# Strassen's seven products for the first matrix product of a feed-forward layer

## The chip, the cores and the metric

The kernel runs on one core of a Trainium2 chip. The metric is the device time of one execution in microseconds (us). The engines of the core are TensorE (PE in the profile; PEld is its weight load), VectorE (DVE), ScalarE (ACT), GpSimd (POOL) and SyncE (SP), which issues DMA transfers. Each works through its own list of instructions in order and waits on semaphores for the others.

## The reference

The program is one step of a hybrid encoder layer for two groups of requests with the same weights: one stream of 512 positions and eight streams of 16, 640 tokens in all. D is 1024, the hidden width 2816. The change touches only the last part of the layer:

```python
hf = rmsnorm(x, lw['norm_ffn'])
u, gf = jnp.split(hf @ lw['w_up'], 2, axis=-1)
gf, f_conv_new = causal_dwconv(gf, f_conv, lw['f_conv_w'], lw['f_conv_b'])
x = x + (u * jax.nn.silu(gf)) @ lw['w_down']
```

The convolution has three taps along the positions; f_conv_new holds each stream's last two inputs of it. A final RMSNorm of x follows.

## The kernel before

**Products in three passes.** Values are float32, and TensorE is given float32r operands. An operand a is held as ah (a rounded, a copy by ScalarE) and al = a − ah (a subtraction). A product is the sum of ah·bh, ah·bl and al·bh, so one product with a contraction of 128 is three matmul instructions. For weights, ScalarE makes wh and GpSimd wl from a raw tile that SyncE's queue loads (512 KB each, tag raw, two buffers; wh and wl have six buffers each, 128x512).

**The FFN.** The 2816 hidden columns are 22 factors f of 128. X is the normed input, transposed, in eight parts k of 128 features by 640 tokens. For each f, fmj makes the gate (fps) and then the up product (ups): eight k, three passes, two halves of 320 tokens, so 48 matmul instructions each, into a pair of PSUM banks (PD, tag D, two buffers of two banks; PP, tag P, has four of one). Behind the gate, conv and silu_conv run: ScalarE copies the PSUM into xp, VectorE does the three taps into xc, ScalarE a tanh, VectorE the gate (fs). Behind the up product, VectorE multiplies fs with ups, and split makes hh (ScalarE) and hl (VectorE). lt collects the last inputs of the convolution for f_conv_new (GpSimd).

After f = 7 and f = 15, add_proj multiplies eight factors by w_down (dn, 240 matmul instructions of 512 columns, through wmj) and adds the result to x; after f = 21, last_proj does the other six and the final norm. For f = 0, fmj (split) does the first 320 tokens ahead of the others, so that it begins before the sample streams (token tile 4) are normed.

**Order.** The program is written in one order; each engine's order comes from a scheduler that follows the program and the buffers, and the semaphores are placed by it. A tile of a pool is given out again when all its readers are done. Dependencies inside a PSUM pair go by the tile.

Of the kernel before, what the change touches and what calls it, by code (L numbers as in the profile page):

```python
# [44 lines left out]
class Enc:  # L45
# [1688 lines left out]
    def ffn(self, x, X):
        I, O = self.I, self.O
        wu, wd = I["w_up"][0], I["w_down"][0]
        lt = None
        for f0, n in ((0, 8), (8, 8), (16, 6)):
            H = []
            for f in range(f0, f0 + n):  # L1740
                nb = 4 if f < 20 else 2
                if f % 4 == 0:
                    lt = self.Q("lt")
                s = []

                def gate(ps, f=f, lt=lt, nb=nb, s=s):
                    s.append(self.silu_conv(ps, "f", f, 2, [self.vc("fcw", i * NFF + f) for i in range(3)],
                                            self.vc("fcb", f), (lt, f % 4, nb), "fs"))
                    yield
                    if f % 4 == nb - 1:  # L1750
                        self.store_conv((lt, 0, nb), [(f - f % 4 + i) * P for i in range(nb)], 2,
                                        O["ffn_conv_prompt"], O["ffn_conv_sample"])

                def up(ps, s=s):
                    t = s[0]
                    sv = t.rearrange("p (a b) -> p a b", a=2)
                    self.tt(sv, sv, ps[:, :, :HALF], ALU.mult)
                    h, l = self.U("hh", F32R), self.U("hl", F32R)
                    self.split(h, l, t)
                    H.append((h, l))  # L1760
                first = f == 0
# [2 lines left out]
            if f0 + n < NFF:
                yield from self.add_proj(wd, H, x, k0=f0, nk=n, nm="dn")
            else:
                yield from self.last_proj(wd, H, x, f0, n)
# [31 lines left out]
    def run(self):  # L1799
        I = self.I  # L1800
        all_ = lambda gen: [None for _ in gen]
        x0 = [self.load_x(0)]
# [140 lines left out]
        _, X = to
        self.drive(self.norm_T(x, g, to, ((0, 1), (2, 3))))
        self.need("WS")
        all_(self.norm_T(x, g, to, ((4,),)))
        all_(self.ffn(x, X))

# [46 lines left out]
```

## Time and profile before

| | us |
|---|---|
| median of 3 runs | 1786.48 |
| lowest and highest | 1783.69, 1791.82 |
| the profiled execution | 1787.08 |
| its span, first to last instruction | 1785.4 |

The span lacks the 1.7 us around the first and last instruction. The FFN fills its end: the first product of f = 0 starts at 1303.0, dn stands at 1422.6 and 1589.9, and the last dn starts at 1729.25.

### The profile page before, as it was taken

What the parts mean: (1) busy time and instruction counts of PE and PEld (TensorE: products, weight loads), DVE (VectorE), ACT (ScalarE), POOL (GpSimd) and SP (SyncE); (2) the same over time, 40 slices, a digit from 0 to 9 for tenths busy, and PEclk for the clock granted to TensorE, in tenths of its full rate; (3) what the DMA queues carried; (4) which work ended last, traced back from release to release, by engine and by line L of the source; (5) the groups of instructions that cost most, each with busy time, mean ns of one, the idle gap of its engine ahead of it and who ended that gap; (6) DMA issues with size and microseconds to landing.
All of it is one profiled execution on the core that took longest, in us unless ns stands there. A gap on an engine that the chain in (4) does not pass through costs nothing.

```text
span 1785.4 us, 32450 instructions
## 1 busy us (share of the span) xinstructions
PE 1683.1 (94%) x12925; PEld 1542.6 (86%) x12925; DVE 860.4 (48%) x1762; ACT 650.5 (36%) x1596; POOL 607.4 (34%) x641
## 2 busy tenths in 40 slices
PE   5898999999999998999999899999889999999997
PEld 4687778898988898998899889987789989998995
DVE  5046762446787674755434463243574404431433
ACT  4234543433434432343342245342443313321332
POOL 3252232123322353453432326201144434443432
PEclk9999999999999999999999999999989999999999
DMA  5332156322222334335323345146332222222221
GB/s 177 89 80 66 40 174 197 131 68 64 78 78 67 109 107 113 85 99 145 84 60 119 106 130 166 59 166 236 114 100 74 83 71 83 72 74 82 72 94 61
DMA packets 232749, 181.78 MB, mean 102 GB/s; under 512 B 14321, under 2 KB 198646, under 8 KB 232470
## 3 DMA queue, kind: packets, MB, share of 16 engines
q1 hardware_dynamic: 210672, 165.74, 30.5%
q10 hardware_dynamic: 21926, 13.96, 2.5%
q8 instruction: 102, 1.67, 0.4%
q14 instruction: 49, 0.40, 0.1%
HBM read 163.09 MB, written 16.06 MB: 100 GB/s over the span
## 4 chain that ended last, share of the span: by engine, by line
PE 69%; DVE 10%; DMA 4%; ACT 3%; issue 2%; POOL 1%; ACTq 0%; SPq 0%; POOLq 0%; DVEq 0%
PE ups L235 9%; PE fps L235 9%; PE gps L235 8%; PE dn L235 8%; PE pps L235 6%; PE ap L235 5%; PE tm L235 4%; PE qps L235 3%; PE cps L235 2%; DVE xc L246 2%; PE bps L235 2%; PE pl L235 1%; DVE t L243 1%; PE py L235 1%; PE xkt L240 1%
## 5 line engine op out<-in xcount | busy, mean ns | idle before, releaser
L243 POOL TENSOR_TENSOR wl<-raw,wh 128x512 fp32r<-128x512 f32 x373 | 490.8, 1321 | 961.3 <-ACT wh L249 791.3
L249 ACT ACTIVATE wh<-raw 128x512 fp32r<-128x512 f32 x400 | 248.8, 629 | 591.0 <-PE fps L235 93.8
L246 DVE SCALAR_TENSOR_TENSOR xc<-xp,vec,xc 128x664 f32<-128x664 f32 (+1 forms) x116 | 117.4, 1012 | 3.2
L235 PE MATMUL gps<-xTh,wh 128*128 128x320 f32 x448 | 117.4, 340 | 0.0
L235 PE MATMUL gps<-xTh,wl 128*128 128x320 f32 x448 | 106.3, 315 | 0.0
L235 PE MATMUL gps<-xTl,wh 128*128 128x320 f32 x448 | 105.6, 315 | 0.0
L568 DVE TENSOR_SCALAR xc<-xp,vec 128x656 f32<-128x656 f32 (+1 forms) x34 | 32.2, 948 | 131.9 <-ACT xp L249 131.9
L235 PE MATMUL dn<-wl,hh 128*128 128x512 f32 x220 | 86.4, 394 | 2.9 <-POOL wl L243 2.6
L235 PE MATMUL dn<-wh,hh 128*128 128x512 f32 x220 | 86.3, 393 | 0.1
L235 PE MATMUL dn<-wh,hl 128*128 128x512 f32 x220 | 85.8, 391 | 0.0
L235 PEld LDWEIGHTS gps<-xTh,wh 128*128 128x128 f32 x448 | 74.1, 192 | 12.0 <-issue 10.8
L235 PE MATMUL fps<-fTh,wh 128*128 128x320 f32 x352 | 82.3, 311 | 0.0
L235 PE MATMUL ups<-fTh,wl 128*128 128x320 f32 x352 | 82.0, 310 | 0.0
L235 PE MATMUL fps<-fTl,wh 128*128 128x320 f32 x352 | 81.9, 310 | 0.0
L235 PE MATMUL fps<-fTh,wl 128*128 128x320 f32 x352 | 81.9, 310 | 0.0
L235 PE MATMUL ups<-fTl,wh 128*128 128x320 f32 x352 | 81.8, 310 | 0.0
L235 PE MATMUL ups<-fTh,wh 128*128 128x320 f32 x352 | 81.7, 310 | 0.0
L235 PEld LDWEIGHTS gps<-xTh,wl 128*128 128x128 f32 x448 | 76.0, 190 | 1.0 <-issue 0.8
L235 PEld LDWEIGHTS gps<-xTl,wh 128*128 128x128 f32 x448 | 76.1, 191 | 0.7 <-issue 0.6
L235 PE MATMUL tm<-wh,xTh 128*128 128x256 f32 (+1 forms) x200 | 65.5, 327 | 8.6 <-ACT wh L249 4.4
L243 DVE TENSOR_TENSOR x<-x,dn 128x512 f32<-128x512 f32 x30 | 19.3, 683 | 108.1 <-PE dn L235 107.7
L235 PE MATMUL tm<-wh,xTl 128*128 128x256 f32 (+1 forms) x200 | 63.6, 318 | 0.2 <-DVE xTl L243 0.2
(521 smaller groups left out, 4434.5 us busy)
## 6 DMA issues: line engine op xcount, KB each, us to landing
raw<-in_w_in_dram SPq DMA_DIRECT2D x72, 512.0 KB
raw<-in_w_up_dram SPq DMA_DIRECT2D x44, 512.0 KB
raw<-in_w_down_dram SPq DMA_DIRECT2D x22, 512.0 KB
ck<-in_cache_attn_k_dram SPq DMA_DIRECT2D x32, 256.0 KB
cv<-in_cache_attn_v_dram SPq DMA_DIRECT2D x32, 256.0 KB
xck<-in_cache_mem_k_dram SPq DMA_DIRECT2D x32, 256.0 KB
xcv<-in_cache_mem_v_dram SPq DMA_DIRECT2D x32, 256.0 KB
raw<-in_wx_o_dram SPq DMA_DIRECT2D x14, 512.0 KB
```

What stands on the lines that cost most here:

```text
L235: self.nc.tensor.matmul(out, lhsT=lhsT, rhs=rhs, start=start, stop=stop)
L240: self.nc.tensor.transpose(out, in_, self.ident[b:b + k, b:b + k])
L243: return (eng or self.nc.vector).tensor_tensor(out, a, b, op=op)
L246: self.nc.vector.scalar_tensor_tensor(out, a, s, b, op0=op0, op1=op1)
L249: self.nc.scalar.activation(out, in_, f, **kw)
L568: nc.vector.tensor_scalar(acc[:, :n], xp[:, :n], taps[0], bias, op0=ALU.mult, op1=ALU.add)
```

## The change

The first product is made by the Winograd form of Strassen's algorithm. The contraction is cut in two (k 0 to 3, 4 to 7), the tokens in two (320 each), and the two rows of blocks are the up columns and the gate columns of one f. Seven products of half the contraction by 320 tokens replace eight, so 84 matmul instructions a factor replace 96. For that:

- ffn_weights loads the two raw tiles of a factor and makes four sums of weights on VectorE (ws: s1 to s4, 128x512); half_w makes h and l of seven operands rather than four.
- norm_S replaces norm_T. It holds three blocks of the normed input (b11, b21, b22) and four sums of blocks (t1 to t4; tile tq) as h and l, made in three groups of token tiles.
- ffn_products makes the seven products, two of them at a time in the halves of an fps pair, three in single banks (fpc). VectorE puts their sums together (fo, fu) and writes the gate straight into xp.
- ffn_gate is the convolution and the gate as a generator in steps, advanced once per product. ScalarE does the first tap. The factors of w_down follow after f = 4, 8, 12 and 16, four at a time, and six at the end.
- ffn makes each weight operand LW = 3 products ahead of its use. The products b11 and b21 of f = 0 and 1 come ahead of the rest.
- wmj takes one PSUM pair and three single banks for its five tiles, where it took two pairs and one.

```diff
+LW = 3
@@ wmj
         tiles = list(tiles)
-        acc = []
-        for i in range(0, len(tiles) - 1, 2):
-            ps = self.PD(nm)
-            acc += [(tiles[i], ps[:, 0]), (tiles[i + 1], ps[:, 1])]
-        if len(tiles) % 2:
-            acc.append((tiles[-1], self.PP(nm)))
+        ps = self.PD(nm)
+        acc = [(t, ps[:, i] if i < 2 else self.PP(nm)) for i, t in enumerate(tiles)]
@@ norm_S
+            groups = ((0, 2), (1, 3), (4,))
+            for gi, tiles in enumerate(groups):
+                if gi == 2:
+                    self.need("WS")
+                r = self.token_norm([x[t] for t in tiles])
+                yield FR
...
+                for n, v in (("b11", b11), ("b21", b21), ("b22", b22)):
+                    h, l = QT[n]
+                    for i in range(2):
+                        self.act(h[i][:, :, s], v[:, 2 * i:2 * i + 2, :])
+                        self.tt(l[i][:, :, s], v[:, 2 * i:2 * i + 2, :], h[i][:, :, s].bitcast(F32), ALU.subtract)
+                T = [self.U("tf", shape=(P, 4, w)) for _ in range(4)]
+                self.act(T[2], b12)
+                self.tt(T[0], T[2], b11, ALU.subtract)
+                self.tt(T[1], b22, T[0], ALU.subtract)
+                self.tt(T[2], b22, T[2], ALU.subtract)
+                self.tt(T[3], b21, T[1], ALU.subtract)
+                for i in (1, 0, 2, 3):
+                    h, l = QT[f"t{i + 1}"]
+                    self.act(h[:, :, s], T[i])
+                    self.tt(l[:, :, s], T[i], h[:, :, s].bitcast(F32), ALU.subtract, nc.gpsimd)
@@ half_w, seven, ffn_weights
+        self.act(h, x)
+        self.tt(l, x, h.bitcast(F32), ALU.subtract, eng or self.nc.gpsimd)
...
+        for k in range(4):
+            (wh, wl), (xh, xl) = w[k], q[k]
+            for p, (a, b) in enumerate(((wh, xh), (wh, xl), (wl, xh))):
+                self.mm(ps, a, b, start=(k == 0 and p == 0), stop=(k == 3 and p == 2))
...
+        up, gate = self.raw(wu, f * P, P, 0, NK), self.raw(wu, FF + f * P, P, 0, NK)
+        a11, a12, a21, a22 = up[:, :4], up[:, 4:], gate[:, :4], gate[:, 4:]
+        s1, s2, s3, s4 = (self.U("ws", shape=(P, 4, P)) for _ in range(4))
+        self.tt(s1, a21, a22, ALU.add)
+        self.tt(s2, s1, a11, ALU.subtract)
+        self.tt(s3, a11, a21, ALU.subtract)
+        self.tt(s4, a12, s2, ALU.subtract)
+        for x in (a11, a12, a22, s2, s3, s1, s4):
+            yield self.half_w(x)
@@ ffn_products
+        ps = self.PD("fps")
+        ps = [ps[:, i, :HALF] for i in range(2)]
+        self.seven(ps[0], W.pop(0), B["b11"])
+        self.act(o[:, 1], ps[0])
+        yield
+        self.seven(ps[1], W.pop(0), B["b21"])
+        self.tt(o[:, 0], ps[1], o[:, 1], ALU.add)
+        yield
+        pc = self.PP("fpc")[:, :HALF]
+        self.seven(pc, W.pop(0), B["t4"])
+        yield
+        u = self.U("fu", shape=(P, 2, HALF))
+        ps = self.PD("fps")
+        ps = [ps[:, i, :HALF] for i in range(2)]
+        self.seven(ps[0], W.pop(0), B["t2"])
+        self.tt(u[:, 0], ps[0], o[:, 1], ALU.add)
+        yield
+        self.seven(ps[1], W.pop(0), B["t3"])
+        self.tt(u[:, 1], ps[1], u[:, 0], ALU.add)
...
+        put(0, pc, u[:, 1])
+        yield
+        ps = self.PP("fpc")[:, :HALF]
+        self.seven(ps, W.pop(0), B["t1"])
+        put(1, ps, u[:, 1])
+        self.tt(o[:, 1], ps, u[:, 0], ALU.add)
+        yield
+        ps = self.PP("fpc")[:, :HALF]
+        self.seven(ps, W.pop(0), B["b22"])
+        self.tt(o[:, 1], ps, o[:, 1], ALU.add)
+        R.append((f, xp, o))
@@ ffn_gate
+        self.act(acc[:, :n], xp[:, :n], AF.Identity, scale=taps[0], bias=self.vc("fcb", f))
+        yield
+        for i in range(1, 3):
+            self.stt(acc[:, :n], xp[:, i:i + n], taps[i], acc[:, :n], ALU.mult, ALU.add)
...
+        yield
+        self.stt(t[:, :512], t[:, :512], 1.0, ap, ALU.add, ALU.mult)
+        self.stt(ts, ts, 1.0, as_, ALU.add, ALU.mult)
+        for v, m in ((t[:, :512], slice(0, 256)), (t[:, 512:], slice(256, HALF))):
+            v = v.rearrange("p (a b) -> p a b", a=2)
+            self.tt(v, v, o[:, :, m], ALU.mult)
+        yield
+        h, l = self.U("hh", F32R), self.U("hl", F32R)
+        self.split(h, l, t)
@@ ffn
-        for f0, n in ((0, 8), (8, 8), (16, 6)):
...
-                yield from self.fmj(lambda: self.weights(wu, FF + f * P, P, 0, NK), X, gate, nm="fps", split=first)
-                yield from self.fmj(lambda: self.weights(wu, f * P, P, 0, NK), X, up, nm="ups", split=first)
+        for n, (f, i) in enumerate(porder):
+            while made < len(worder) and made < max(n + 1 + LW, len(first)):
+                wf = worder[made][0]
+                if wf not in G:
+                    G[wf] = self.ffn_weights(wf)
+                W[wf].append(next(G[wf]))
+                made += 1
+            if f not in pr:
+                pr[f] = self.ffn_products(f, W[f], B, R)
+            next(pr[f])
+            chains = [c for c in chains if next(c, self) is not self]
+            if R:
+                c = self.ffn_gate(*R.pop(), H, lts)
+                next(c)
+                chains.append(c)
+            if i == 6 and f % 4 == 0 and 0 < f < 20:
+                all_(self.add_proj(wd, H[done:], x, k0=done, nk=4, nm="dn"))
+                done += 4
```

The first place is VectorE's list in one steady factor. A row has the line, the operation, output and inputs, the size, and the engines or DMA queues for which it waits (Activation is ScalarE). Before, a factor is these seven rows:

```order
L568 TENSOR_SCALAR xc_15985<-xp_15977,vec_668 128x656 [waits Activation_49]
L246 SCALAR_TENSOR_TENSOR xc_15985<-xp_15977,vec_668,xc_15985 128x656 [waits DVE_49] x2
L554 COPY xp_16606<-st_f 128x8x2 [waits DVE_49,Pool_49]
L246 SCALAR_TENSOR_TENSOR fs_15989<-fs_15989,xc_15985 128x512 [waits Activation_49]
L246 SCALAR_TENSOR_TENSOR fs_15989<-fs_15989,xc_15985 128x128 [waits Activation_49]
L243 TENSOR_TENSOR fs_15989<-fs_15989,ups_15994 128x640 [waits DVE_49,PE_49]
L243 TENSOR_TENSOR hl_16055<-fs_15989,hh_16054 128x640 [waits Activation_49]
```

In the changed kernel the stretch from the gate of one factor to the sum that ends the next factor's t3 reads:

```order
L243 SCALAR_TENSOR_TENSOR fs_16494<-fs_16494,xc_16471 128x512 [waits Activation_49]
L243 SCALAR_TENSOR_TENSOR fs_16494<-fs_16494,xc_16471 128x128 [waits Activation_49]
L240 TENSOR_TENSOR fs_16494<-fs_16494,fo_16477 128x512 [waits DVE_49]
L240 TENSOR_TENSOR fs_16494<-fs_16494,fo_16477 128x128 [waits DVE_49]
L240 TENSOR_TENSOR fo_16477<-fps_16478,fo_16477 128x320 [waits PE_49]
L240 TENSOR_TENSOR hl_16536<-fs_16494,hh_16535 128x640 [waits Activation_49,Pool_49]
L240 TENSOR_TENSOR fu_16543<-fps_16544,fo_16477 128x320 [waits PE_49]
L240 TENSOR_TENSOR ws_16562<-raw_16560 128x512 [waits DMAHW3_49,Pool_49]
L240 TENSOR_TENSOR ws_16563<-ws_16562,raw_16558 128x512 [waits DMAHW2_49,DVE_49,Pool_49]
L240 TENSOR_TENSOR ws_16564<-raw_16558,raw_16560 128x512
L240 TENSOR_TENSOR ws_16565<-raw_16558,ws_16563 128x512 [waits DVE_49]
L240 TENSOR_TENSOR fu_16543<-fps_16544,fu_16543 128x320 [waits PE_49]
```

The sum fu of the product t2 has moved behind the previous factor's gate and hl, and the four sums of weights stand between it and the sum of t3; the two puts in two rows each, two more sums into fo and two taps make the rest of the factor.

The second place is TensorE's list in the same factor, in the changed kernel: the end of t2 (fps_16544, first half), the five instructions of t1 (fpc_16596) and the start of t3 (second half of the same pair).

```order
L232 MATMUL fps_16544<-tqh_14767,wl_16474 128x320
L232 MATMUL fpc_16596<-tqh_14767,wh_16518 128x320 [waits DVE_49,PE_49]
L232 MATMUL fpc_16596<-tql_14769,wh_16518 128x320
L232 MATMUL fpc_16596<-tqh_14767,wl_16519 128x320 [waits Pool_49]
L232 MATMUL fpc_16596<-tqh_14767,wh_16518 128x320
L232 MATMUL fpc_16596<-tql_14769,wh_16518 128x320
L232 MATMUL fps_16544<-tqh_14768,wh_16497 128x320 [waits DVE_49]
L232 MATMUL fps_16544<-tql_14770,wh_16497 128x320
```

Before, these were 96 instructions in a row that wait for weights only. Now t3 waits for VectorE, for the sum fu that reads the other half of its pair.

The third place is VectorE's list at the FFN's start, behind the last sum of x (x_11238). Before, what follows is four splits of the transposed input (fTl), the norm of tile 4, and its two splits:

```order
L243 TENSOR_TENSOR x_11238<-x_11238,ap_14943 128x256 [waits PE_49]
L243 TENSOR_TENSOR fTl_14753<-nps_14989,fTh_14751 128x4x128 [waits Activation_49]
L243 TENSOR_TENSOR fTl_14754<-nps_14998,fTh_14752 128x4x128 [waits Activation_49]
L243 TENSOR_TENSOR fTl_14753<-nps_15007,fTh_14751 128x4x128 [waits Activation_49]
L243 TENSOR_TENSOR fTl_14754<-nps_15016,fTh_14752 128x4x128 [waits Activation_49]
L243 TENSOR_TENSOR v_15028<-ss_15023 128x1 [waits Activation_49]
```

In the changed kernel the sums of the first group of tiles and the whole norm of the second stand there; this is the beginning, and 13 rows 128x2 wide (v to y) follow the first of them, before the four xn, six splits and four sums of that group and then tile 4's:

```order
L240 TENSOR_TENSOR x_11238<-x_11238,ap_14924 128x256 [waits PE_49]
L240 TENSOR_TENSOR tf_14976<-tf_14978,nps_14839 128x512 [waits DMAHW7_49,Activation_49]
L240 TENSOR_TENSOR tf_14977<-nps_14952,tf_14976 128x512 [waits DVE_49]
L240 TENSOR_TENSOR tf_14978<-nps_14952,tf_14978 128x512
L240 TENSOR_TENSOR tf_14979<-nps_14886,tf_14977 128x512 [waits DVE_49]
L240 TENSOR_TENSOR v_15002<-ss_14993 128x2 [waits Activation_49]
```

The norm of tile 4 has moved behind the second group's norm, and every product now reads all token tiles.

## Rows read from the trace of the kernel before

**Rows 1.** The page: busy us of each engine, its share of the span, instructions.

```profile
PE 1683.1 (94%) x12925; PEld 1542.6 (86%) x12925; DVE 860.4 (48%) x1762; ACT 650.5 (36%) x1596; POOL 607.4 (34%) x641
```

**Rows 2.** Windows: length; busy us PE, PEld, DVE, ACT, POOL; clock, DMA share, GB/s.

```profile
1303.00:1323.80 20.80, 17.02 (x108) 16.65 (x107) 13.50 (x25) 7.91 (x17) 9.22 (x9) 0.92 0.33 98
...
1337.90:1422.60 84.70, 84.70 (x580) 84.64 (x579) 37.46 (x49) 29.07 (x62) 35.08 (x42) 1.00 0.25 76
```

**Rows 3.** The chain that ended last: start, us, what; FFN and last dn.

```profile
1415.45 7.04 PE ups L235 x48
1422.60 54.43 PE dn L235 x240
...
1729.25 18.60 PE dn L235 x81
```

**Rows 4.** Groups by form (busy, mean ns, idle before), 1337.9 to 1422.6.

```profile
L246 DVE SCALAR_TENSOR_TENSOR xc<-xp,vec,xc 128x656 f32<-128x656 f32 x12 | 10.8, 902 | 0.4
L246 DVE SCALAR_TENSOR_TENSOR fs<-fs,xc 128x512 f32<-128x512 f32 x6 | 8.5, 1409 | 2.5 <-ACT fs L249 2.5
...
L243 DVE TENSOR_TENSOR fs<-fs,ups 128x640 f32<-128x640 f32 x7 | 5.8, 822 | 5.1 <-PE ups L235 5.1
L243 DVE TENSOR_TENSOR hl<-fs,hh 128x640 fp32r<-128x640 f32 x6 | 5.0, 829 | 7.4 <-ACT hh L249 7.4
L246 DVE SCALAR_TENSOR_TENSOR fs<-fs,xc 128x128 f32<-128x128 f32 x6 | 1.7, 279 | 0.0
...
L249 ACT ACTIVATE wh<-raw 128x512 fp32r<-128x512 f32 x25 | 15.8, 632 | 51.7 <-PE fps L235 25.2 <-PE ups L235 13.5 <-POOL lt L560 13.0
L249 ACT ACTIVATE hh<-fs 128x640 fp32r<-128x640 f32 x6 | 4.4, 741 | 5.1 <-DMA out_dram<-cso 2.8 <-DVE fs L243 2.3
...
L243 POOL TENSOR_TENSOR wl<-raw,wh 128x512 fp32r<-128x512 f32 x24 | 31.3, 1303 | 38.6 <-ACT wh L249 38.3
L559 POOL COPY lt<-xp 128x2 f32<-128x2 f32 x6 | 2.7, 457 | 0.0
```

**Rows 5.** Groups of VectorE over the span: one PSUM operand.

```profile
L243 DVE TENSOR_TENSOR x<-x,dn 128x512 f32<-128x512 f32 x30 | 19.3, 683 | 108.1 <-PE dn L235 107.7
...
L243 DVE TENSOR_TENSOR x<-x,ap 128x256 f32<-128x256 f32 x40 | 15.4, 417 | 39.6 <-PE ap L235 38.9 <-DMA x<-in_x_prompt_dram 0.6
```

**Rows 6.** Timeline of VectorE, then GpSimd, in one steady factor.

```profile
1349.69 1.61 DVE L246 SCALAR_TENSOR_TENSOR fs<-fs,xc 128x512 f32<-128x512 f32 x2 [0.42 <-ACT fs L249]
...
1353.65 0.83 DVE L243 TENSOR_TENSOR hl<-fs,hh 128x640 fp32r<-128x640 f32 x1 [0.81 <-ACT hh L249]
...
1349.25 1.30 POOL L243 TENSOR_TENSOR wl<-raw,wh 128x512 fp32r<-128x512 f32 x1
```

**Rows 7.** Timeline at the first factor: VectorE, then GpSimd.

```profile
1301.16 0.42 DVE L243 TENSOR_TENSOR x<-x,ap 128x256 f32<-128x256 f32 x1
...
1305.28 1.12 DVE L243 TENSOR_TENSOR t<-y,w 128x1 f32<-128x1 f32 x1
...
1308.93 1.19 DVE L243 TENSOR_TENSOR t<-y,w 128x1 f32<-128x1 f32 x1
1310.15 0.16 DVE L243 TENSOR_TENSOR t<-t,y 128x1 f32<-128x1 f32 x1
...
1311.12 1.41 DVE L246 SCALAR_TENSOR_TENSOR xn<-x,y,grow 128x512 f32<-128x512 f32 x2
...
1305.09 5.01 POOL L243 TENSOR_TENSOR wl<-raw,wh 128x512 fp32r<-128x512 f32 x4 [2.74 <-DVE y L498]
```

**Rows 8.** The same, some 10 us later: VectorE, then GpSimd.

```profile
1321.48 1.84 DVE L246 SCALAR_TENSOR_TENSOR xc<-xp,vec,xc 128x656 f32<-128x656 f32 x2
...
1322.71 1.76 POOL L243 TENSOR_TENSOR wl<-raw,wh 128x512 fp32r<-128x512 f32 x1 [1.09 <-ACT wh L249]
```

**Rows 9.** The chain, where the last product before the FFN waited for weights.

```profile
1292.12 3.54 DMA raw<-in_wx_o_dram
...
1296.45 1.28 POOL wl L243
```

More of the change, by code (lines that the diff above doesn't have):

```diff
@@ L1731, in cross_sample @@
         return scores(), out()
[L1734 to L1737, printed above, removed]
-        for f0, n in ((0, 8), (8, 8), (16, 6)):
[L1739 to L1761, printed above, removed]
-                yield from self.fmj(lambda: self.weights(wu, FF + f * P, P, 0, NK), X, gate, nm="fps", split=first)
-                yield from self.fmj(lambda: self.weights(wu, f * P, P, 0, NK), X, up, nm="ups", split=first)
[L1764 to L1767, printed above, removed]
@@ new lines, in norm_S, with steps @@
+    def norm_S(self, x, gain):
+        nc = self.nc
+        QT = {}
+        for n in ("b11", "b21", "b22"):
+            QT[n] = [[self.U(n + a, F32R, (P, 2, HALF)) for _ in range(2)] for a in "hl"]
+        big = [[self.xp4.tile([P, 2, 4, HALF], F32R, name=self.nm("tq" + a), tag="X", bufs=4) for _ in range(2)]
+               for a in "hl"]
+        for i, n in enumerate(("t1", "t2", "t3", "t4")):
+            QT[n] = [big[a][i // 2][:, i % 2] for a in range(2)]
+        ops = {n: [(q[0][k // 2][:, k % 2, :], q[1][k // 2][:, k % 2, :]) if n[0] == "b" else
+                   (q[0][:, k, :], q[1][:, k, :]) for k in range(4)] for n, q in QT.items()}
+        def steps():
+            groups = ((0, 2), (1, 3), (4,))
[4 more added lines that the diff above has]
+                yield FR
+                pss = [[None, None], [None, None]]
+                for i, t in enumerate(tiles):
+                    for j, ps in self.norm_tile(x[t], r[:, i:i + 1], gain):
+                        if len(tiles) == 2:
+                            pss[j][i] = ps
+                        else:
+                            pss[j] = [ps[:, :, :64], ps[:, :, 64:]]
+                        yield FR
+                (b11, b12), (b21, b22) = pss
+                w = b11.shape[2]
+                s = slice(gi * P, gi * P + w)
+                for n, v in (("b11", b11), ("b21", b21), ("b22", b22)):
[13 more added lines that the diff above has]
+                    self.tt(l[:, :, s], T[i], h[:, :, s].bitcast(F32), ALU.subtract, nc.gpsimd)
+                yield FR
+        return ops, steps()
@@ new lines, in half_w, with seven @@
+    def half_w(self, x, eng=None, loose=False):
+        h, l = (self.U("w" + a, F32R, (P, 4, P)) if loose else
+                self.wp.tile([P, 4, P], F32R, name=self.nm("w" + a), tag="w" + a) for a in "hl")
+        self.act(h, x)
+        self.tt(l, x, h.bitcast(F32), ALU.subtract, eng or self.nc.gpsimd)
+        return [(h[:, k, :], l[:, k, :]) for k in range(4)]
+    def seven(self, ps, w, q):
+        for k in range(4):
+            (wh, wl), (xh, xl) = w[k], q[k]
+            for p, (a, b) in enumerate(((wh, xh), (wh, xl), (wl, xh))):
+                self.mm(ps, a, b, start=(k == 0 and p == 0), stop=(k == 3 and p == 2))
@@ new lines, in ffn_gate @@
+    def ffn_gate(self, f, xp, o, H, lts):
+        nc, O = self.nc, self.O
+        hist, step, base = 2, 18, 514
+        nb = 4 if f < 20 else 2
+        if f % 4 == 0:
+            lts.append(self.Q("lt"))
+        lt, i = lts[-1], f % 4
+        nc.gpsimd.tensor_copy(lt[:, i * hist:(i + 1) * hist], xp[:, 512:512 + hist])
+        nc.gpsimd.tensor_copy(
+            lt[:, (nb + 8 * i) * hist:(nb + 8 * i + 8) * hist].rearrange("p (b c) -> p b c", c=hist),
+            xp[:, 512 + step:512 + 9 * step].rearrange("p (b c) -> p b c", c=step)[:, :, :hist])
+        n = base + 8 * step - hist
+        acc = self.xpp.tile([P, 684], F32, name=self.nm("xc"), tag="xc")
+        taps = [self.vc("fcw", i * NFF + f) for i in range(3)]
+        self.act(acc[:, :n], xp[:, :n], AF.Identity, scale=taps[0], bias=self.vc("fcb", f))
+        yield
+        for i in range(1, 3):
+            self.stt(acc[:, :n], xp[:, i:i + n], taps[i], acc[:, :n], ALU.mult, ALU.add)
+        ap, as_ = acc[:, :512], acc[:, base:base + 8 * step].rearrange("p (b c) -> p b c", c=step)[:, :, :16]
+        t = self.U("fs")
+        ts = t[:, 512:].rearrange("p (b c) -> p b c", c=16)
+        self.act(t[:, :512], ap, AF.Tanh)
+        self.act(ts, as_, AF.Tanh)
+        yield
[4 more added lines that the diff above has]
+            self.tt(v, v, o[:, :, m], ALU.mult)
+        yield
+        h, l = self.U("hh", F32R), self.U("hl", F32R)
+        self.split(h, l, t)
+        H.append((h, l))
+        if f % 4 == nb - 1:
+            self.store_conv((lt, 0, nb), [(f - f % 4 + i) * P for i in range(nb)], 2,
+                            O["ffn_conv_prompt"], O["ffn_conv_sample"])
@@ new lines, in ffn @@
+    def ffn(self, x, B):
+        wd = self.I["w_down"][0]
+        H, lts, R = [], [], []
+        all_ = lambda gen: [None for _ in gen]
+        W = {f: [] for f in range(NFF)}
+        G = {}
+        first = [(0, 0), (0, 1), (0, 2), (1, 0), (1, 1), (1, 2)]
+        worder = first + [(f, i) for f in range(2) for i in range(3, 7)] + \
+            [(f, i) for f in range(2, NFF) for i in range(7)]
+        porder = [(0, 0), (0, 1), (1, 0), (1, 1)] + [(f, i) for f in range(2) for i in range(2, 7)] + \
+            [(f, i) for f in range(2, NFF) for i in range(7)]
+        made = 0
+        pr, chains = {}, []
+        done = 0
+        for n, (f, i) in enumerate(porder):
[16 more added lines that the diff above has]
+                done += 4
+        for c in chains:
+            all_(c)
+        all_(self.last_proj(wd, H[done:], x, done, NFF - done))
@@ L1940, in run @@
         self.need("WL")
-        to = self.XT("fT")
         g = self.grow(I["norm_ffn"][0])
[L1943 to L1947, printed above, removed]
+        B, norm = self.norm_S(x, g)
+        self.drive(norm)
+        self.ffn(x, B)
 _INS = ['x_prompt', 'x_sample', 'cache_attn_k', 'cache_attn_v', 'state_b_conv', 'state_b_rec', 'state_c_conv',
```

14 lines of the change are left out of this document (added).

## Prediction

> **What bounds the kernel now.** I read the page first: TensorE is busy 94% of the span [rows 1]. A share of the whole span hides stages, so the windows come next, cut at the FFN's boundaries. In a steady stretch of six factors TensorE is busy 84.70 of 84.70 us, while VectorE has 37.5, ScalarE 29.1 and GpSimd 35.1 [rows 2]. The chain of waits says the same: 48 products in 7.04 us, and dn 54.43 us long, begun 0.1 us after the last up product [rows 3]. So 96 products cost 14.08 us a factor (146.6 ns each), and every other engine has more than half of its time free. Only the first two factors are ragged: from 1303.0 to 1337.9 stand 28.16 us of products in 34.9 us, with a granted clock of 0.92 up to 1323.8; in the steady stretch it is 1.00, the upper of its two levels, 2.4 GHz [rows 2].
>
> Strassen makes 84 products of 96: 12.31 us, 1.77 us less a factor, 38.8 us over 22. That would be the gain if TensorE stayed the bound. The question is whether VectorE, GpSimd and ScalarE now fit into 12.31 us a factor.
>
> **The new work a factor, by rows.** GpSimd makes seven l halves in place of four: 7 x 1.30 = 9.1 us, and the two lt copies, of which the row of the first has 0.46 [rows 4]; ScalarE seven h halves at 0.63 and hh at 0.74 as the rows have them, and, estimated from these rows by width, tanh at 0.63 and 0.29, the first tap of the convolution at 0.75 and fo at 0.42: about 7.3 us. Neither alone fills 12.3.
>
> VectorE: a row with one PSUM operand costs 0.417 us at 256 columns and 0.683 at 512 [rows 5], which is 0.151 + 0.00104 a column. Estimated from that, the five sums at 320 columns (fo twice from b21 and b22, once from t1, fu twice) take 5 x 0.484 = 2.42, the four puts 2 x (0.417 + 0.218) = 1.27: 3.69 us. Sums of two SBUF operands: two convolution taps 1.80, the gate's two rows (512 at the same 0.683, 128 at 0.28) 0.96, the product with u again 0.96, hl 0.83, and the four new weight sums s1 to s4 4 x 0.683 = 2.73: 7.28 us [rows 4, 5]. VectorE is busy 10.97 us. It is in order and on its list waits for ScalarE twice a factor, for tanh (0.63 and handovers, some 0.75) and for hh (hl starts after 0.81 of idle time) [rows 6]: 12.5 us a factor in a row, already TensorE's 12.3.
>
> **VectorE is on the path, by false dependencies.** In the order, t3 (second half of an fps pair) waits for VectorE's fu sum of the first half, and fu stands behind the previous factor's gate, its hl and the sum of b21, with s1 to s4 behind it in turn. What lies between t2 and t3 is five products of t1, 0.73 us. So each factor TensorE waits until VectorE has come round once: the period is the longer of 12.31 and VectorE's round. Lead in the weights (LW = 3) does not loosen this, since fu is about products, not weights.
>
> **VectorE and GpSimd exclude each other.** This is the dear term. Four one-column rsqrt rows in a row (the first and the last are shown), which take 0.16 us alone, took 1.1 to 1.2 us each while GpSimd made four l's back to back [rows 7]: one VectorE row got in after each l. The gate's pair ran 1.61 us where it began 0.44 us into an l [rows 6], ending 0.75 us after that l; its larger row averages 1.409 us in the steady stretch [rows 4], against 0.68 for its size. GpSimd suffers likewise: an l begun in the middle of the two taps took 1.76 and ended 1.15 us after them [rows 8]. Sums with a PSUM operand do not show it: fs<-fs,ups at 640 columns stays at 0.82 [rows 4].
>
> The Trainium skill states the rule: SBUF — State Buffer, section "Who interferes with whom", says that VectorE and GpSimd share a pair of ports under an exclusive lock, and that a VectorE instruction with two SBUF inputs contends there with a GpSimd instruction that reads SBUF. The trace agrees: 1.2 us for 0.16, and 0.82 unchanged with a PSUM operand. Without the lock VectorE's round would be the 12.5 us above.
>
> So per factor 7 x 1.15 = 8.05 us of GpSimd must fall outside VectorE's 7.28. VectorE leaves 12.5 − 7.28 = 5.2 us: sums with PSUM operands, and its waits. If all of that is filled, 2.8 us remain: 15.3. By the 0.75 us in which the gate's pair was done after an l (0.96 alone, so some 22% of such a row overlaps the end of the other engine's), 1.6 us come back: 13.7, the best. If an l falls at random, 7.28/12.5 = 58% of 8.05 is lost: 17.2, the worst. GpSimd runs ahead while VectorE waits, but is held in its own order by the lt copies and by slots that TensorE frees, so I take T = 15.5, near the first.
>
> **The sum over 20 steady factors.** Before: 20 x 14.08 = 281.6. After: the four that follow a dn begin with their convolution done beneath it, so they take about 12.75; 16 take T. 51 + 16 x 15.5 = 299, **+17.4 us** (T = 13.7: −11.4; 17.2: +44.6).
>
> **The dn boundaries.** The products in dn are as many as before, cut five ways for three. In the order, the first raw of a dn is behind the four weight sums and the l of a next-factor half, because the two raw buffers are still read by them. Its DMA lands 3.54 us after issue in the one place where the chain waited for a raw, then wh at 0.63 and an l of 1.28: 5.5 us [rows 4, 9]. It is issued some 2 to 4 us after fu, with t3, t1's last seven and b22 (4.5 us) still to run. Stall 1 to 4.5 us, five times, where before the first such gap is 0.1 [rows 3]: 2.5 each, **+12** (5 to 22).
>
> **The start.** Before, TensorE began f = 0 at 1303.0 on tiles 0 to 3, the last sum of x having landed at 1301.6. After, every product spans all 640 columns and waits for tile 4, whose norm now stands at the end of a longer list. From 1301.6 on VectorE has, in order: four sums of group one (2.7), 13 one-column rows (2.5 alone, 6.3 if four are blocked as in [rows 7]), four xn at 0.70 (2.8), six b halves that each wait for ScalarE (2.5 to 4), four sums (2.7), 13 one-column rows (2.5 to 6.3), two xn (1.4), and tile 4's transposes and first split (2.4). That is 19.5 to 28.6; I take 22.5, first product at 1324. Two factors at 13 us end at 1350, against 1337.9: **+12** (8 to 20). The half-wide wmj (one pair and three singles) moves nothing: its sums of x are the same.
>
> The tail's six factors of w_down remain as they are: 56 us from its first product to the span's end [rows 3].
>
> **Sum.** 17.4 + 12 + 12 = +41. The profiled execution took 1787.08 us (span 1785.4), 0.6 above the median; 1787.1 + 41 = **1828**.
>
> **Rivals.**
> TensorE-bound (faster): the lock costs little since GpSimd's l's slide into VectorE's waits of themselves and the round is 12.5. For it: PSUM rows are free of the lock. Against: 1.409 for 0.68 with only four l's a factor. 51 + 16 x 12.6 − 281.6 = −29; with the start at +9 and the boundaries at +5, −15: **1772**. It decides in favour of the change if T is below about 13.2.
> Even: T = 13.7 with well-packed handovers, −11, start +8, boundaries +5: +2, **1789**.
> Worse: T = 17.2, +45, start +18, boundaries +16: **1866**. The clock could add to this: with gaps, 1303 to 1323.8 was granted 0.92, and 1.2 GHz in the gaps would lengthen what follows.
> That the change does nothing is excluded, since the list of products is different.
>
> **Chances.** Forecast 0.60, worse 0.18, even 0.11, TensorE-bound 0.11. Half a per cent, 8.9 us, is about what a measurement of this kernel tells from no change. Faster 0.12, same 0.10, slower 0.78; the likeliest case's own range is 1800 to 1855. Leaving out a tenth at each side, the range is 1788 to 1870.
>
> **What the changed profile would show.** Right: TensorE some 79% busy in the steady factors, its idle time put down to VectorE's fu at t3; factors 15 to 16 us apart; s1 to s4 and the taps well above 0.683 and 0.90 in the mean, PSUM sums near 0.48; the first product near 1324; gaps of 1 to 4 us at each dn, after a raw. Wrong: factors 12.3 to 13 us apart with TensorE full, which would say that two-operand rows and l's pass each other; or waits for l in the steady stretch, which would make GpSimd, not VectorE's list, the bound.

## Result and the profile after

The changed kernel takes 1860.91 us (median of 4 runs, 1859.19 to 1862.22) against 1788.2 for the kernel before (4 runs): a ratio of 1.0407, 95% interval 1.0380 to 1.0435. It is slower by 72.7 us, as the spans say too (1858.1 against 1785.4); 1828 had been forecast. The page of its profiled execution, with the row of busy time to set beside [rows 1], and the granted clock in 40 slices:

```profile
PE 1679.8 (90%) x12661; PEld 1524.7 (82%) x12661; DVE 1039.4 (56%) x2066; ACT 702.6 (38%) x1663; POOL 740.8 (40%) x741
...
PEclk8999999999999999999999999999698999999999
```

TensorE is busy only 3 us less, though the FFN's first product takes an eighth fewer matmul instructions. Part of them ran at the lower of the clock's two levels, as the windows show (columns as in [rows 2]): the first of two gaps ahead of the first product; factors 0 and 1; 2 to 4; four factors with their dn; of these, the second factor, a piece of the third, the first 4 us of the dn and the whole of it.

```profile
1299.98:1311.08 11.10, 0.00 (x0) 0.03 (x1) 7.62 (x21) 5.53 (x14) 7.97 (x7) 0.50 0.12 36
...
1326.06:1364.49 38.43, 30.34 (x170) 28.39 (x169) 25.50 (x41) 15.28 (x32) 26.05 (x23) 0.84 0.20 55
...
1364.49:1419.09 54.60, 43.01 (x256) 41.22 (x254) 46.16 (x69) 21.20 (x39) 33.34 (x35) 0.91 0.27 78
...
1541.09:1633.39 92.30, 81.91 (x458) 74.40 (x457) 60.07 (x92) 32.49 (x57) 55.14 (x52) 0.96 0.23 69
...
1553.66:1568.95 15.29, 12.85 (x86) 12.32 (x85) 13.81 (x21) 6.66 (x12) 11.45 (x12) 1.00 0.25 70
...
1579.64:1585.84 6.20, 6.20 (x32) 6.20 (x32) 5.84 (x10) 1.86 (x3) 4.83 (x4) 0.72 0.21 59
...
1603.94:1608.00 4.06, 3.66 (x9) 2.63 (x10) 0.00 (x0) 1.10 (x2) 3.93 (x5) 0.62 0.11 24
...
1603.94:1633.39 29.45, 29.05 (x120) 23.61 (x121) 4.92 (x9) 5.52 (x9) 12.98 (x12) 0.94 0.23 72
```

Where the 72.7 us are: the third factor begins at 1364.5 in place of 1337.9, **+26.6**. From there to the last dn there are 438.9 us (to 1803.3) in place of 391.4 (1337.9 to 1729.25 [rows 3]), **+47.5**: 92.3 us for four factors and a dn, three times, against 4 x 14.08 + 27.2 = 83.5. The tail is 1.4 shorter. The wait table of TensorE from the third factor to the last dn (waiting place, releaser: total us, times, longest) shows the two waits that were forecast, for fu at t3 and for the first weights of dn:

```profile
PE fps L232 <- DVE fu L240: 33.1, 16, 4.1
PE dn L232 <- ACT wh L246: 13.1, 4, 4.0
PE fps L232 <- ACT fo L246: 4.5, 10, 0.9
```

The groups of VectorE and GpSimd in 17 factors (1448.7 to 1803.3), to be read against [rows 4, 5]:

```profile
L243 DVE SCALAR_TENSOR_TENSOR xc<-xp,vec,xc 128x656 f32<-128x656 f32 x34 | 44.0, 1293 | 1.8 <-ACT xc L246 0.7
L240 DVE TENSOR_TENSOR ws<-ws,raw 128x512 f32<-128x512 f32 x16 | 22.2, 1387 | 1.1 <-issue 0.4
L240 DVE TENSOR_TENSOR ws<-raw 128x512 f32<-128x512 f32 x16 | 21.8, 1361 | 0.0
L240 DVE TENSOR_TENSOR fs<-fs,fo 128x512 f32<-128x512 f32 x17 | 20.4, 1197 | 0.0
...
L243 DVE SCALAR_TENSOR_TENSOR fs<-fs,xc 128x512 f32<-128x512 f32 x17 | 16.3, 958 | 18.4 <-ACT fs L246 18.4
...
L240 DVE TENSOR_TENSOR ws<-raw,raw 128x512 f32<-128x512 f32 x16 | 10.9, 681 | 0.0
...
L240 DVE TENSOR_TENSOR fu<-fps,fo 128x320 f32<-128x320 f32 x17 | 8.3, 486 | 0.0
...
L240 POOL TENSOR_TENSOR wl<-raw,wh 128x512 fp32r<-128x512 f32 x78 | 110.7, 1427 | 84.0 <-ACT wh L246 84.0
L240 POOL TENSOR_TENSOR wl<-ws,wh 128x512 fp32r<-128x512 f32 x66 | 98.9, 1514 | 44.1 <-ACT wh L246 43.9 <-issue 0.2
```

Rows with two SBUF operands are stretched (taps 1.29 for 0.90, weight sums up to 1.39 for 0.68), those with a PSUM operand are not (fu 0.486, estimated 0.484); GpSimd's l halves are stretched as well (1.43 and 1.51 for 1.30). In the timeline of one factor, VectorE and then GpSimd, the first two sums give way to two l's and the next two, with GpSimd idle, do not:

```profile
1564.17 1.37 DVE L240 TENSOR_TENSOR ws<-raw 128x512 f32<-128x512 f32 x1
1565.57 1.68 DVE L240 TENSOR_TENSOR ws<-ws,raw 128x512 f32<-128x512 f32 x1
1567.17 0.68 DVE L240 TENSOR_TENSOR ws<-raw,raw 128x512 f32<-128x512 f32 x1
1567.77 0.68 DVE L240 TENSOR_TENSOR ws<-raw,ws 128x512 f32<-128x512 f32 x1
...
1563.59 3.11 POOL L240 TENSOR_TENSOR wl<-raw,wh 128x512 fp32r<-128x512 f32 x2 [2.12 <-ACT wh L246]
```

### The profile page after: what moved, and what is told of

The parts are those of the page before. It is cut to its first block, busy times and chain, and to the rows that moved or that the text cites. A ratio compares the mean times of both kernels' runs of the same rounds, so it can differ in the third digit from the quotient of the medians.

```text
span 1858.1 us, 32581 instructions
## 1 busy us (share of the span) xinstructions
PE 1679.8 (90%) x12661; PEld 1524.7 (82%) x12661; DVE 1039.4 (56%) x2066; ACT 702.6 (38%) x1663; POOL 740.8 (40%) x741
## 5 line engine op out<-in xcount | busy, mean ns | idle before, releaser
L240 POOL TENSOR_TENSOR wl<-raw,wh 128x512 fp32r<-128x512 f32 x351 | 475.7, 1363 | 852.5 <-ACT wh L246 676.9
L246 ACT ACTIVATE wh<-raw 128x512 fp32r<-128x512 f32 x378 | 232.6, 627 | 428.0 <-PE dn L232 69.8
L240 POOL TENSOR_TENSOR wl<-ws,wh 128x512 fp32r<-128x512 f32 x88 | 130.1, 1494 | 57.7 <-ACT wh L246 53.2
L243 DVE SCALAR_TENSOR_TENSOR xc<-xp,vec,xc 128x664 f32<-128x664 f32 (+1 forms) x116 | 135.6, 1169 | 4.8 <-ACT xc L246 1.7
L232 PE MATMUL dn<-wh,hh 128*128 128x512 f32 x220 | 88.2, 401 | 13.2 <-ACT wh L246 13.1
L246 ACT ACTIVATE wh<-ws 128x512 fp32r<-128x512 f32 x88 | 53.8, 627 | 104.6 <-PE dn L232 33.5
L232 PE MATMUL fps<-tqh,wh 128*128 128x320 f32 x176 | 60.1, 342 | 34.5 <-DVE fu L240 34.5
L232 PEld LDWEIGHTS gps<-xTh,wh 128*128 128x128 f32 x448 | 74.1, 192 | 12.0 <-issue 10.9
L232 PEld LDWEIGHTS fps<-tqh,wh 128*128 128x128 f32 x176 | 35.2, 200 | 39.7 <-DVE fu L240 39.0
L237 PE MATMUL nps<-ident,xn 128*128 128x128 f32 x136 | 27.2, 351 | 43.4 <-DVE xn L243 43.3
L232 PE MATMUL tm<-wl,xTh 128*128 128x256 f32 (+1 forms) x200 | 64.3, 322 | 0.1
L232 PEld LDWEIGHTS dn<-wh,hh 128*128 128x128 f32 x220 | 42.4, 193 | 23.8 <-ACT wh L246 14.3
```

Source lines behind the costliest of these rows:

```text
L232: self.nc.tensor.matmul(out, lhsT=lhsT, rhs=rhs, start=start, stop=stop)
L237: self.nc.tensor.transpose(out, in_, self.ident[b:b + k, b:b + k])
L240: return (eng or self.nc.vector).tensor_tensor(out, a, b, op=op)
L243: self.nc.vector.scalar_tensor_tensor(out, a, s, b, op0=op0, op1=op1)
L246: self.nc.scalar.activation(out, in_, f, **kw)
```

## Experiments

All start from the changed kernel; times are of one run unless a count is given (the changed kernel's own four runs span 3.0 us). A factor's time is from its first product (b11) to the next one's; a cycle is four factors and their dn.

**1. No subtraction on GpSimd.**

```diff
-        self.tt(l, x, h.bitcast(F32), ALU.subtract, eng or self.nc.gpsimd)
+        self.nc.gpsimd.memset(l.bitcast(F32), 0.0)
```

> In the changed kernel a steady factor (the second after a dn) takes 15.29 us and four factors with their dn 92.3. Here GpSimd fills the low halves of the FFN's weights with zeros instead of subtracting, so that part of the products is left out: GpSimd still issues seven instructions a factor, but they read nothing from SBUF. Theory (VectorE's two-operand rows and GpSimd's subtractions exclude each other, and VectorE's round is the period): the taps fall from 1.17 us in the mean to 0.90, the weight sums to 0.68, a steady factor to 12.3 to 12.8, the kernel to 1805 to 1820. Rival 1 (VectorE's list is simply too long, whatever GpSimd does): list and waits are untouched, a steady factor stays at 15 and the kernel at 1855 to 1862. Rival 2 (GpSimd's own load): the period falls as well, but the taps' and sums' mean times stay as they are.

1800.58 us, a factor 12.6, a cycle 81.7. The groups in 17 factors, and the cycle's window:

```profile
L243 DVE SCALAR_TENSOR_TENSOR xc<-xp,vec,xc 128x656 f32<-128x656 f32 x34 | 31.7, 934 | 2.5 <-ACT xc L246 1.8
...
L240 DVE TENSOR_TENSOR fs<-fs,fo 128x512 f32<-128x512 f32 x17 | 11.7, 687 | 0.0
L240 DVE TENSOR_TENSOR ws<-ws,raw 128x512 f32<-128x512 f32 x16 | 11.1, 692 | 0.6
...
L1792 POOL MEMSET wl<- 128x512 f32 x114 | 60.0, 526 | 147.3 <-PE fps L232 103.5 <-PE dn L232 25.1 <-PE fpc L232 18.8
...
1428.70:1510.40 81.70, 79.57 (x458) 72.77 (x457) 45.81 (x91) 32.43 (x57) 27.14 (x52) 0.98 0.27 78
```

VectorE's list is the same, but its rows fall back to their own length and its busy time in a cycle from 60.07 to 45.81. The list alone is not too long: rival 1 is out. The zeros are shorter than the subtractions (0.53 for 1.30), so GpSimd's load fell too. That the load is not what stretches the rows is seen from the mean times, which rival 2 would have left alone; that it does not set the period either is seen in 9, where GpSimd is busy 53.01 us in a cycle of 80.5. The Trainium skill says the same (SBUF — State Buffer, "Who interferes with whom"): a VectorE instruction with two SBUF inputs does not contend with a GpSimd instruction that only writes SBUF. The trace agrees: the weight sums and the gate take 0.69 us beside the zeros. The kernel is still slower than before: the third factor begins at 1359.1, and each dn waits.

**2. Three zeros, four subtractions.** The same edit for the halves of a11, a12 and a22 only.

> Of the seven low halves of a factor, GpSimd fills three (those of the raw quarters) with zeros and subtracts the other four, so part of the products is left out. Seven subtractions gave 15.3 us for the second factor after a dn and 92.3 for four factors with their dn, none gave 12.6 and 81.8. Theory (each subtraction that meets VectorE's two-operand rows costs VectorE up to 1.15 us): the two-operand rows still wait, but fewer; the second factor 12.6 to 13.9, four factors 84 to 89, the kernel 1812 to 1840. Rival (exclusion acts only once GpSimd and VectorE together pass the period, 4 x 1.15 + 12.5 - 5.2 < 12.5): as with no subtraction, 82 for four and 1800 to 1806.

1809.12 us, a factor 12.9, a cycle 82.9:

```profile
1436.50:1519.40 82.90, 80.01 (x458) 72.79 (x457) 49.57 (x92) 33.13 (x57) 43.09 (x52) 0.98 0.26 77
```

Between the two, nearer the rival: against experiment 1, four subtractions a factor add 3.8 us of VectorE time a cycle, seven add 14.3. The first 16 of a cycle cost little, as if they fit into what VectorE leaves open (5.2 us a factor by the forecast, for 4 x 1.15 = 4.6); the other 12 cost 10.5 of their 12 x 1.15 = 13.8 us. These are two points, and which rows the subtractions meet differs between them.

**3. A PSUM bank for each product.**

```diff
-        ps = self.PD("fps")
-        ps = [ps[:, i, :HALF] for i in range(2)]
+        ps = [self.PD("fps")[:, 0, :HALF], self.PP("fpc")[:, :HALF]]
```

> Each of the seven products has a PSUM tile of its own, so t3 no longer waits for the sum fu of t2, nor b21 for the copy of b11. Theory (the period is VectorE's round): TensorE's idle time moves to another wait and a steady factor stays at 15.0 to 15.6, the kernel at 1850 to 1865. Rival (the false dependency inside a PSUM pair is what stops TensorE): a steady factor falls to 12.5 to 13.5 and the kernel to 1810 to 1830.

1859.83 us: the total is as the theory has it, the place is not quite. Two factors after a dn now take 12.3 us and the third 16.6; the cycle stays at 92.4, VectorE's busy time in it at 59.5. TensorE's waits in that cycle:

```profile
PE dn L232 <- ACT wh L246: 6.0, 1, 6.0
PE fpc L232 <- DVE fu L240: 4.1, 2, 2.5
PE fpc L232 <- ACT cso L246: 1.7, 1, 1.7
```

So the false dependency, taken away alone, moves TensorE's waits and does not shorten them in total. They gather before dn, whose first raw tile is issued at 1597.87, when VectorE has ended the fourth weight sum (1597.79): a late list of VectorE reaches TensorE there too. VectorE's busy time over a cycle is not itself the limit: with a third raw buffer (7) it is as long, 60.06 us, and the cycle is 5 us shorter.

**4. Weight sums off VectorE.**

```diff
-        self.tt(s1, a21, a22, ALU.add)
...
+        for s, a in ((s1, a21), (s2, a11), (s3, a22), (s4, a12)):
+            self.act(s, a)
```

> The four weight sums of a factor are copies on ScalarE instead of sums on VectorE, which leaves the sums out of the computation: VectorE loses 4 x 0.68 us a factor, all of it rows with two SBUF operands, ScalarE gains 4 x 0.63. Theory (VectorE's round with GpSimd's exclusions): round 12.5 - 2.7 = 9.8, the remaining 4.6 us of two-operand rows and 8.05 of GpSimd leave TensorE nearly free, a steady factor 12.4 to 13.2, the kernel 1805 to 1825. Rival 1 (the pair's false dependency): fu of t2 stands ahead of the sums in VectorE's list, so a steady factor stays above 14.5. Rival 2 (ScalarE, now some 9.8 us a factor and in order, becomes the bound): 13.5 to 14.5.

1851.22 us, factors of 14.45 and 14.52, a cycle of 90.49: a miss by the theory, on the border of the two rivals. The cycle, and waits of VectorE and TensorE in the first of these factors:

```profile
1537.30:1627.79 90.49, 81.71 (x458) 73.86 (x457) 45.88 (x76) 41.49 (x73) 51.06 (x52) 0.96 0.24 70
...
DVE fu L240 <- PE fps L232: 2.1, 1, 2.1
...
PE fps L232 <- DVE fu L240: 1.6, 1, 1.6
```

VectorE is busy no longer than in experiment 1 (45.88 for 45.81), where a cycle took 81.7, so its busy time alone does not set the period. Its round still does, as the first rival has it: t3 waits for fu of t2 (1.6), VectorE then waits for t3 (2.1), and taps, gate and hl stand between this and the next fu of t2. Without the pair's dependency (5) three factors of four take 12.3. The theory's round of 9.8 us had left the wait for t3 out.

**5. Both edits, 3 and 4.**

> The four weight sums as copies on ScalarE (the sums are left out) and a PSUM tile for each product, the two edits that left a steady factor at 14.5 and, over four factors, unchanged when made alone. Theory (two things in series set the period: VectorE's round with GpSimd's exclusions, and the loop from t3 back to t3 through fu, the taps, the gate and hl, which the pair's false dependency closes): with both gone a steady factor takes 12.3 to 12.8 us and the kernel 1805 to 1825. Rival (ScalarE with its four more rows, or GpSimd, holds the weights back): 13.5 to 14.5 a factor, 1840 to 1852.

1857.50 us, a miss: three factors at 12.3 each, but 25.1 for the fourth with its wait for dn; the cycle is 92.0. Its window, and VectorE's groups of one cycle (1500 to 1590):

```profile
1536.90:1628.90 92.00, 80.26 (x458) 73.19 (x457) 51.42 (x75) 39.66 (x73) 51.81 (x52) 0.94 0.24 70
...
L243 DVE SCALAR_TENSOR_TENSOR xc<-xp,vec,xc 128x656 f32<-128x656 f32 x8 | 13.2, 1649 | 6.1 <-ACT xc L246 3.7 <-POOL wl L240 2.4
...
L240 DVE TENSOR_TENSOR fs<-fs,fo 128x512 f32<-128x512 f32 x4 | 6.0, 1507 | 0.0
L243 DVE SCALAR_TENSOR_TENSOR fs<-fs,xc 128x512 f32<-128x512 f32 x4 | 5.2, 1299 | 4.4 <-ACT fs L246 4.4
```

16 sums of 0.68 are gone, 10.9 us of the 45.8 that VectorE is busy in experiment 1, so 34.9 would be left; it is busy 51.42. GpSimd's subtractions are as many as before and now fall on the taps (1.65 for 0.90) and the gate (1.51 and 1.30 for 0.69). Their toll, the time by which they lengthen VectorE's rows, is 16.5 us a cycle here, 11.0 in 4 with the same rows, and 14.3 in the changed kernel: it depends on which rows meet a subtraction. My sum had counted a row that is removed as time given back.

At the boundary the rival is right as well. ScalarE's copies stand behind its eight DMA issues, the first raw of dn is issued when the fourth copy ends, and dn starts at 1507.1 after a wait of 7.3:

```profile
1497.82 2.66 ACTq L252 DMA_DIRECT2D out_dram<-cso  x8
1500.52 2.19 ACT L246 ACTIVATE ws<-raw 128x512 f32<-128x512 f32 x4 [2.73 <-issue]
...
1502.78 7.27 SPq L249 DMA_DIRECT2D raw<-in_w_down_dram  x3
```

How much of the long fourth factor is ScalarE's and how much the toll's was not separated.

**6. The gate in PSUM.** Single banks as in 3 (all from tag P), and the tile of tanh and gate in a PSUM pair:

```diff
-        t = self.U("fs")
+        t = self.PD("fs").rearrange("p a b -> p (a b)")[:, :TOK]
```

> The whole computation: each product has a single PSUM bank, and the tile of tanh and gate (fs) moves from SBUF into a pair of PSUM banks. VectorE then has the two gate rows, the two products with u and hl with one SBUF operand each: 2.75 us a factor leave the set that excludes GpSimd, 4.5 us (taps, weight sums) remain in it. Theory: with 8.0 us of VectorE's round open to GpSimd's 8.05, a steady factor takes 12.6 to 14.0, 92.4 us for four factors with dn fall to 82 to 88, the kernel 1808 to 1840. Rival (VectorE's round is long by its row count, or PSUM rows cost as much): 15, and 1850 or more.

1828.62 us, within the forecast: factors of 12.3, 13.3 and 12.4, then 5.7 us of waiting before dn. VectorE's groups, and the cycle:

```profile
L243 DVE SCALAR_TENSOR_TENSOR fs<-fs,xc 128x512 f32<-128x512 f32 x4 | 2.8, 700 | 3.2 <-ACT fs L246 3.2
L240 DVE TENSOR_TENSOR fs<-fs,fo 128x512 f32<-128x512 f32 x4 | 2.8, 699 | 0.1
...
1525.30:1612.90 87.60, 80.25 (x458) 73.60 (x457) 52.90 (x92) 32.33 (x57) 52.01 (x52) 0.96 0.25 73
```

The same rows on the same values, with one operand moved to PSUM, take 0.70 in place of 0.96 and 1.20 us, their length without subtractions in 1 (0.69), and VectorE is busy 52.90 us a cycle where 3 had 59.5.

**7. The boundary: a third raw buffer** (bufs=3 for tag raw). In the changed kernel the first raw of dn is issued when VectorE's fourth weight sum ends:

```profile
1597.64 1.79 DVE L240 TENSOR_TENSOR ws<-raw,ws 128x512 f32<-128x512 f32 x1
...
1599.50 7.38 SPq L249 DMA_DIRECT2D raw<-in_w_down_dram  x3
```

First with two tiles fewer in U:

> Three raw buffers in place of two, paid for by two tiles fewer in the pool U (39). Theory (a dn waits 4 us because its first raw is issued only when the fourth weight sum is done): the gap before dn falls from 4.0 to under 1 us, dn runs at the full clock again (27.2 to 27.6 in place of 28.3), each of five boundaries 3 to 5 us shorter, the kernel 1838 to 1848. Rival (the wait is for slots of wh or for ScalarE's place in order): gap of 3 to 4 remains, the kernel within 3 us of 1861.

1857.01 us, a miss by the total. The boundaries went as the theory has it (cycles 86.3 to 87.4), but the smaller pool moved the first group's norm behind the attention part, and the first product came at 1345.0. So again, with eight tiles fewer in pool Q and the start as it was (third factor at 1364.6):

> Three raw buffers again, now paid for by the small tiles of another pool (8 of 16), since the start of the run with two fewer U tiles had changed: there the first group's norm no longer fitted under the attention part. Theory: start as in the changed kernel (third factor at 1364 +- 2), boundaries as in the run before (four factors with their dn 86 to 88 in place of 92.3), the kernel 1836 to 1844. Rival (the shorter boundaries came from the two missing U tiles or from the later start): four factors at 91 to 93, 1855 to 1862.

1841.61 us, cycles of 86.4 to 87.6. dn now runs without a gap ahead of it, at the clock's upper level and in 27.2 us:

```profile
1505.00:1532.20 27.20, 27.20 (x122) 22.51 (x121) 7.25 (x12) 5.58 (x9) 12.15 (x12) 1.00 0.35 112
```

against 29.45 and a gap of 4.0 in the changed kernel. So the late raw cost a boundary some 5 us of the cycle's 92.3, with VectorE busy as long as before (60.06 us a cycle).

**8. The start.** The token norm of the next group ahead of the transposes (r = rn, as in norm_T):

> norm_S takes the token norm of the next group of tiles ahead of the transposes of the present one, as norm_T did; nothing else differs. In the changed kernel the first product stands at 1326.1 and the third factor begins at 1364.5. Theory (VectorE's serial list after the last sum of x sets the start): first product at 1314 to 1320, third factor at 1352 to 1358, the kernel 6 to 12 us shorter, 1849 to 1855. Rival (what follows the first product, low granted clock and late t1 to t4, sets the third factor): first product earlier, the third factor by under 3 us, the kernel 1857 to 1861.

1854.19 us. The first product stands at 1322.4, 3.7 us earlier and not the 6 to 12 expected, the third factor at 1362.2, 2.3 earlier: nearer the rival. The total lies in the theory's range for a reason that the theory did not have: another 2.8 came at one boundary, where the wait was shorter (TensorE's wait, and the dn behind it):

```profile
PE dn L232 <- ACT wh L246: 2.7, 1, 2.7
...
1508.00:1536.10 28.10, 27.66 (x121) 22.58 (x122) 4.93 (x9) 5.56 (x9) 13.00 (x12) 1.00 0.27 83
```

Then TensorE kept busy before the first product:

```diff
+                if gi < 2:
+                    q = QT["b11"][0][0]
+                    for _ in range(45):
+                        ps = self.PP("fill")[:, :256].rearrange("p (a b) -> p a b", a=2)
+                        self.mm(ps, q[:, 0, s], q[:, :, s])
+                    self.act(self.SM("fl", [P, 1]), ps[:, 0, :1])
```

> 90 extra products of 256 columns, whose results nobody reads, fill TensorE's two gaps between the last product of the attention part (1300) and the FFN's first (1326), 45 in each. Theory (low granted clock after idle time is a part of the 38 us that the first two factors take): granted clock of 1326 to 1343 rises from about 0.6 to 1.0, the first twelve products take 1.9 to 2.1 us in place of 3.1, the third factor begins 2 to 5 us earlier, the kernel 1854 to 1859. Rival (late h and l halves of t1 to t4 and of the weights set it): products faster, the third factor within 1.5 us of 1364.5.

1869.11 us, inconclusive, so the clock's share in the start is not shown by a run of its own: the row that reads the filler's result stands in ScalarE's list ahead of the next squares, so it held the norm back (first product 1335.2), and the clock did not rise either: 0.62 while TensorE was busy 12 of 14 us.

```profile
1312.00:1326.00 14.00, 11.99 (x45) 9.52 (x46) 8.13 (x18) 4.95 (x11) 5.02 (x4) 0.62 0.00 0
```

**9. Together.** Edits 6, 7 (with eight Q tiles fewer) and the first of 8:

> The whole computation, with four edits to the changed kernel: single PSUM banks for the products, tanh and gate in a PSUM pair, the token norm of the next group ahead, three raw buffers (8 small tiles fewer). If their gains add up: 1828.6 less 3 to 7 for the norm and 16 to 24 for the boundaries, 1798 to 1810, still slower than the kernel before since the start costs 20 us. Rival (they remove the same waits, so the gains overlap): 1815 to 1828.

1792.93 us (10 runs), 1.0029 of the kernel before (1787.41; interval 1.0016 to 1.0041): less than the 1798 to 1810 of the parts added up. With the first two factors' b11 in PD (free there), and one yield ahead of store_conv:

> The whole computation, the run before with two more edits: b11 of the first two factors in the pair tile that is still free there, so that TensorE's fourth product no longer waits 4.9 us for ScalarE's copy of the first, and the store of the convolution's inputs one step later, so that its transpose does not wait 0.8 us for GpSimd's lt copy, five times. Theory (both waits end last where they stand): third factor at 1351 to 1353 in place of 1356.1, each boundary 0.5 to 0.9 shorter, the kernel 1784 to 1789, level with the kernel before. Rival (behind each of these waits stands another of like length): 1790 to 1793.

1786.41 us (12 runs) against 1790.57 (17 runs): a ratio of **0.9976 (0.9964 to 0.9987)**. That is level with the kernel before or a quarter of a per cent faster; the kernel before itself took 1787.41 beside the previous run. The third factor begins at 1350.6, still 12.7 later than before, and a cycle is 80.5 us, three less than before, at the upper clock:

```profile
1497.80:1578.30 80.50, 77.53 (x459) 71.80 (x458) 51.89 (x92) 32.31 (x57) 53.01 (x52) 1.00 0.26 79
```

## Why the prediction was right, and where it fell short

**The number.** +41 was forecast and +72.7 measured. The direction and the mechanism were right, the size was not: 1860.9 lies inside the outer range (1788 to 1870), but above the likeliest case's own (1800 to 1855), and near the rival "worse" (1866), though T was not that rival's 17.2. Of some 31 us between forecast and result, 14.6 are at the start and 18.1 between the third factor and the last dn (+47.5 for 17.4 and 12); the tail gives 1.4 back.

**The mechanism held.** VectorE's round with GpSimd's exclusions became the period: TensorE's waits are for fu, and taking the subtractions away (1) brings a factor to 12.6, the forecast's own value without the lock. Experiment 6 shows the same from VectorE's side. T had been put at 15.5; the second factor takes 15.29, and the three after a first one (12.57) take 15.3, 16.9 and 14.1 in a cycle, 15.4 in the mean. Part of this agreement is luck: 0.5 of the 15.4 is the lower clock in the third factor (32 products busy 6.20 us, at 146.6 ns each 4.69), which T did not hold. And factors 2 to 4, ahead of the first dn, took 16.2, 18.5 and 18.7 us without the wait for dn, 6.9 more than three times 15.5. Factors 3 and 4, with gaps of 4.1 and 2.9 us in them:

```profile
1380.67:1399.15 18.48, 14.32 (x87) 13.79 (x85) 15.92 (x25) 6.81 (x12) 11.63 (x13) 0.91 0.30 84
1399.15:1419.09 19.94, 15.84 (x88) 15.09 (x86) 15.60 (x22) 7.44 (x14) 9.20 (x12) 0.83 0.26 83
```

The reading of T as what is left after the open 5.2 us agrees with four subtractions (2). Its use for a changed list failed in 4 and 5: 10.9 us of rows taken away shortened the cycle by 1.8 and 0.3 us, and VectorE's waits for t3 and for ScalarE were missing from the round.

**The boundaries** were put at +12, as five waits of 2.5. The waits come to 13.1 us at four of them (1.2, and 3.9 to 4.0 three times), near the forecast. What was mis-sized is dn itself, forecast as before: each of the four ran 2.2 to 2.4 us longer than its 27.2, 9.2 us together. Three cycles of 92.3 stand against the 88.95 of the forecast (12.75 + 3 x 15.5 + 2.5 + 27.2).

**The start was mis-sized most**: +12, measured +26.6. The first product was near (1326.1 for 1324): VectorE's list is the one given, with few blocked rows but with two waits of 3.0 and 1.8 us for ScalarE's squares. But two factors were then put at 13 us each, 26, and took 38.4: 24.6 of products at full clock, some 5.7 because TensorE ran part of them at the lower level (busy 30.34), and 8.1 of waits for weights, for the halves of t1 to t4 and for fu.

**The term that was missing** is the clock, named in the rival "worse" and left out of the sum. After gaps of 10 us, of 2.9 to 4.1, and at one factor in some cycles of 2.1, TensorE was granted 0.50 to 0.74 for a while. [rows 2] had shown it (0.92 up to 1323.8) without a price. Nor was the number of waits after the first product taken into the sum; before, the products of tiles 0 to 3 ran meanwhile.

## What to carry to other kernels

Saving products on TensorE by sums elsewhere is paid in the engines that make and split the operands: add up, per period, what VectorE does with two SBUF operands and what GpSimd reads from SBUF as one resource, before comparing either with TensorE. That sum leaves out VectorE's waits, and which rows meet decides what the meeting costs. Moving one operand of such rows to PSUM gave them their own length back and the kernel 31 us (6 against 3); taking 10.9 us of other rows out of a cycle shortened it by 1.8 and 0.3 us (4, 5). And price a stall twice, for its length and for what TensorE may run at the lower clock after it.

## What the runs showed of the hardware that was not expected

The toll is not in proportion to GpSimd's work: VectorE's busy time in a cycle was 45.81, 49.57 and 60.07 us with none, four and seven subtractions a factor. Nor is it in proportion to VectorE's list: with a quarter of that gone (34.9 us left) VectorE was busy 45.88 in experiment 4 and 51.42 in 5, with the same rows and as many subtractions.

The length of a gap alone does not say what it costs. Ahead of a dn, a gap of 4.0 us in the changed kernel was followed by 0.62 in the first 4 us and a dn of 29.45; one of 2.7 (experiment 8, at 1508.0) by 1.00 and 28.1. Yet gaps of 2.1 us were followed by 0.58 and 29.0 in experiment 1 (at 1563.3) and by 1.00 and 28.1 in experiment 2 (at 1573.0). What else decides stays open.
